# Split values written by 16 transfers of full rows; the inverse's transposes and the first preparation's sums tied to places in TensorE's row

## The chip, the cores and the metric

The kernel runs on one core of a Trainium2 chip. The metric is the device time of one execution in microseconds (us). Runs of one kernel agree to about 0.2%, some 3 us here.

## What is computed

One layer of a diffusion backbone: 1024 latent tokens and 256 context tokens, width 1024, batch 1. The normalised, modulated tokens go through one input projection, whose columns feed two groups; their outputs are projected back, and a SwiGLU network follows.

```python
px = modulate(rms_norm(x, norm1_w), sh1, sc1) @ w_in      # latent
pc = modulate(rms_norm(ctx, norm1_w), csh1, csc1) @ w_in  # context
# group A: gated DeltaNet, 4 heads of 128, forward and backward, chunks of 64
qkv = short_conv(p[..., :3 * DN_WIDTH], conv_w)           # 5 taps, then SiLU
m = jnp.where(strict, jnp.einsum("bhncd,bhnmd->bhncm", kb, k) * decay, 0.0)
a_mat = jnp.eye(CHUNK) + m
u = triangular_solve(a_mat, v * beta); w = triangular_solve(a_mat, kb * jnp.exp(gam))
qk = jnp.where(tril, jnp.einsum("bhncd,bhnmd->bhncm", q, k) * decay, 0.0)
# ... scan over the chunks, then per-head rms_norm * silu(z)
# group B: 8 heads of 64, windows of 8 rows x 16 columns on a 64-wide grid, plus all context keys
s = jnp.concatenate([s_win, s_ctx], axis=-1)
o = softmax(s) @ (v of the window and of the context)
x = x + g1 * (jnp.concatenate([dn_x, na_x], axis=-1) @ w_out)
x = x + g2 * swiglu(modulate(rms_norm(x, norm2_w), sh2, sc2), w_ffn_in, w_ffn_out)
```

## The kernel before

**Products.** Operands in float32 are split into a high and a low part, and each product is three: high by high, low by high, high by low. The tokens' parts are `hh` and `hl`, a weight's `whi` and `wlo`. ACT casts a weight's high part, POOL subtracts to get the low one (L198 and L199 for a block; L584 and L585 for a wide job).

**Jobs.** The input projection is a list of jobs. A *block* computes 128 columns of one kind with columns on partitions: k, q, v of group A (with convolution and SiLU) or nk, nq of group B. For each of 8 slices of the width it issues three products for two or three segments of tokens (L404, up to 512 tokens each). Its life goes on while later jobs run: evacuation from the accumulators by ACT (L452), the convolution on DVE (L456, L460), SiLU on ACT (L467), norm (sums on TensorE at L485 or L491, then L492, L496, L499), finish (transposes on TensorE at L526 for v, and stores). A *wide* job has tokens on partitions, its weights are loaded in two halves through one raw buffer (`wraw`, one copy; load L583, then L584 and L585), and its products are L592, 24 for a tile of 128 tokens. The kinds are z1, nv0, nv1 and z0. The list is k0 to k3, z1, nk0 to nk2, nv0, nk3, q0 to q3, nq0 to nq3, v0, nv1, v1, v2, v3, z0. The weights of a job are requested while the job before it is traced; z0, the last, runs beside the beginning of group B's attention (scores L302, biases L304, exponential L306, transposes L313, values L323).

**Values.** The nv jobs (two halves of the columns) store the values of group B to `nv_d` in device memory (L603). After each, SP issues 64 transfers that sort them by column block into `vw_d` (L1104), 32 KB each, in pieces of 512 bytes. The attention loads one piece of 1536 bytes per partition for each tile (L277).

**Background.** Python generators step beside the jobs, some steps to a slice. `block_inverses` builds decay tables and inverts the triangular blocks: transposes on TensorE (L870), a back-substitution on DVE (L880 and L882, 30 rounds, then the memset of the diagonal, L885), a pause of some steps, then transposes back (L892, 8 groups of 4, of which two are printed as one row of 8, with copies by ACT at L894), a DVE transpose and a scaling (L900, L903), and stores to `x_d`. Then `preps` prepares 10 chunks for both directions, two of them at a time: tables `rg` on POOL (L952), sums on TensorE (L964, L965), exponential (L968), products with the keys on DVE (L971), copies of 32x32 blocks to `y` on POOL (L974), products L984 and L995 with evacuations by ACT and DVE (L987, L997, L998), stores (L1007).

**What sets the order.** The program is traced once; a scheduler then sets the row in which each engine takes its instructions, by data and by its own estimates of when things are ready, and each engine works its row strictly in order. `tc.keep_in_program_order(x)` holds an instruction behind all that was traced before it on its engine. DMA queues are fed by SP and ACT in their rows too.

Of the kernel before, what the change touches and what calls it, by code (L numbers as in the profile page):

```python
# [88 lines left out]
def hybrid(ctx, tc, a, dbg):  # L89
# [56 lines left out]
    nv_d = dram.tile([T, 512], F32, name="nv_d", tag="nv_d")  # L146
    nq_d = dram.tile([NAH, 2, ND, L], F16, name="nq_d", tag="nq_d")
    nk_d = dram.tile([2, NAH, ND, T], F16, name="nk_d", tag="nk_d")
    vw_d = dram.tile([128, 4, 4, 4, 128], F32, name="vw_d", tag="vw_d")
    y_d = dram.tile([2, NCH, 128, 4, 128], F32, name="y_d", tag="y_d")  # L150
    at_d = dram.tile([2, 8, 128, 4, 128], F32, name="at_d", tag="at_d")
    x_d = dram.tile([128, 2, 2, NU, 32], F32, name="x_d", tag="x_d")
# [100 lines left out]
    def attention(nw):  # L253
# [20 lines left out]

        def values(hp, half, cb):
            vw = nw.tile([128, 3, 128], F32, name="vw", tag="vw", bufs=3)
            sp.dma_start(vw, vw_d[:, hp, cb, half:half + 3])  # L277
            return vw

        def context(hp):  # L280
# [93 lines left out]
    with ExitStack() as bs:  # L374
# [445 lines left out]
        def block_inverses():  # L820
            with ExitStack() as gs:
# [61 lines left out]
                    yield  # L883
                flat = N.rearrange("p b r c -> p b (r c)")
                dve.memset(flat[:P, :, 0:1024:33], 1.0)  # L885
                for _ in range(4):
                    yield
                U = WK.rearrange("p d u i -> p (d u) i")
                for i0 in range(0, 32, 4):
                    p = bank()  # L890
                    for i in range(4):
                        pe.transpose(p[:, i * P:(i + 1) * P], N[:P, :, :, i0 + i].rearrange("p b r -> p (b r)"),  # L892
                                     ident[:P, :P])
                    act.copy(U[:, :, i0:i0 + 4], p[:, :4 * P].rearrange("p (i u) -> p u i", i=4))  # L894
                    if i0 % 8 == 4:
                        yield
# [15 lines left out]
        def preps():  # L912

            first_half.close()
            with ExitStack() as gs:
                pk = pools(gs, "pk", "left")
                shift(gs, "ppad", "left", 64)
                pp = pools(gs, "pp", "left")

                def work(name, bufs=2, dt=F32):  # L920
                    return (pk if name == "kk" else pp).tile([128, 4, 128], dt, name=name, tag=name, bufs=bufs)

                fxs = [work(f"fx{d}", 1) for d in range(2)]
                ys = [[work(f"y{d}{i}", 1) for d in range(2)] for i in range(2)]
                for t in fxs + ys[0] + ys[1]:
                    pool.memset(t, 0.0)
                q32 = [slice(b * 32, b * 32 + 32) for b in range(4)]

                def fetch(i):

                    got = []
                    for d in range(2):
                        c = ORDER[d][i]
                        kk, xc = work("kk", 6), pp.tile([128, 2, 4, 32], F32, name="xc", tag="xc", bufs=4)
                        sp.dma_start(kk, kk_d[:, c])
                        sp.dma_start(xc, x_d[:, d, :, c * 4:c * 4 + 4])
                        at = None
                        if c >= 2:
                            at = work("at", 4)
                            sp.dma_start(at, qk_d[:, c - 2])  # L940
                        got.append((d, c, kk, xc, at))
                    return i, got

                def prep(i, got):
                    y = ys[i % 2]
                    rgs = []
                    for d, c, kk, xc, at in got:
                        mle = M[C_LE + d].rearrange("p (o i) -> p o i", o=1).to_broadcast([128, 4, 128])
                        for gg in (GH, GL):
                            rg = work("rg", 4, F32R)  # L950
                            g = gg.bitcast(F32)[:, d, c].rearrange("p (h o) -> p h o", o=1).to_broadcast([128, 4, 128])
                            pool.tensor_tensor(rg, g, mle, OP.mult)  # L952
                            rgs.append(rg)
                    for d, c, kk, xc, at in got:
                        for q in q32:
                            act.copy(fxs[d][q, :, q], xc[q, 1])
                    yield 1
                    if i == 0:
                        yield 1
                    es = []  # L960
                    for d, c, kk, xc, at in got:
                        p = bank("pr")
                        for j in range(2):
                            pe.matmul(p, mr[:, d], fl(rgs[2 * d + j]), start=j == 0, stop=False)  # L964
                        pe.matmul(p, mr[:, 4], mneg[:, d].rearrange("p (o i) -> p o i", o=1).to_broadcast(  # L965
                            [128, 4, 128]), start=False, stop=True)
                        e = work("e", 2)
                        act.activation(fl(e), p, AF.Exp)  # L968
                        es.append(e)
                    for (d, c, kk, xc, at), e in zip(got, es):  # L970
                        dve.tensor_tensor(kk, kk, e, OP.mult)  # L971
                    for (d, c, kk, xc, at), e in zip(got, es):
                        for q in q32:
                            pool.tensor_copy(y[d][q, :, q], xc[q, 0])  # L974
                        if at is not None:
                            dve.tensor_tensor(at, at, e, OP.mult)
                            stores.append((at_d[d, c - 2], at, tick[0] + 2))
                    yield 1
                    yield 1
                    ps = []  # L980
                    for d, c, kk, xc, at in got:
                        p = bank("pr")
                        for h in range(4):
                            pe.matmul(p[:, hs[h]], kk[:, h], fxs[d][:, h], start=True, stop=True)  # L984
                        ps.append(p)
                    for (d, c, kk, xc, at), p in zip(got, ps):
                        act.copy(fl(kk), p)  # L987
                    yield 1
                    for n in range(1, 4):
                        blk = (q32[3 - n], q32[n])  # L990
                        cols = (slice(128 - 32 * n, 128), slice(0, 32 * n))
                        ps = [bank("pr").rearrange("p (h i) -> p h i", h=4) for _ in got]
                        for h in range(4):
                            for (d, c, kk, xc, at), p in zip(got, ps):
                                pe.matmul(p[blk[d], h, :32 * n], kk[:, h, blk[d]], y[d][:, h, cols[d]],  # L995
                                          start=True, stop=True)
                        dve.tensor_copy(y[0][blk[0], :, cols[0]], ps[0][blk[0], :, :32 * n])  # L997
                        act.copy(y[1][blk[1], :, cols[1]], ps[1][blk[1], :, :32 * n])  # L998
                        yield 1
                    for d, c, kk, xc, at in got:  # L1000
                        stores.append((y_d[d, c], y[d], tick[0] + 1))

                stores, tick = [], [0]

                def flush(n):
                    while stores and stores[0][2] <= n:
                        sp.dma_start(*stores.pop(0)[:2])  # L1007

                todo = list(range(NCH))
                live, landing = [], []  # L1010
                while live or todo or landing:
                    if not landing and todo and (todo[0] < 2 or all(x in done for x in queries)):
                        landing.append(fetch(todo.pop(0)))
                    if landing and (not live or len(live) < 2 and live[0][1] >= 4):
                        live.append([prep(*landing.pop(0)), 0])
                    if not live:
                        yield
                    for g in list(live):
                        tick[0] += 1
                        flush(tick[0])  # L1020
                        g[1] += 1
                        if not next(g[0], 0):
                            live.remove(g)
                        yield
                flush(tick[0] + 2)
# [23 lines left out]
        for n in range(2, len(jobs) + 2):  # L1049
# [44 lines left out]
            for _ in fin:  # L1094
                pass
            done.add(n - 2)
            if isinstance(j, Wide) and j.kind == "nv":
                hv = slice(2 * j.half, 2 * j.half + 2)
                vlat = nv_d[CT:].rearrange("(r c) d -> r c d", c=64)
                for cb in range(4):  # L1100
                    for ch in range(4):
                        for r in range(4):
                            rows = vlat[4 * ch + r, BLKS[cb]:BLKS[cb] + 32].rearrange("c (h d) -> c h d", d=128)
                            sp.dma_start(vw_d[r * 32:r * 32 + 32, hv, cb, ch], rows[:, hv])  # L1104
            if nrm:
                nrm.norm()
            if isinstance(j, Block):
# [665 lines left out]
```

## Time and profile before

| | us |
|---|---|
| median of three runs (1541.44 to 1543.45) | 1541.6 |
| the profiled execution | 1541.49 |
| its span, first to last instruction | 1539.4 |
| mean granted TensorE clock | 0.988 |
| PE waiting for DVE at the statistics of the start (L717) | 9.9 |
| transfers L1104: issued from 215.4 to 521.3 | 128 of some 0.6 each |

The profile is of one execution. PE is TensorE, DVE VectorE, ACT ScalarE, POOL GpSimd, SP the engine that issues most transfers; the "q" forms are their sequencers. A timeline row gives the start, the time, the engine, line, operation, output and inputs, the tile, the count, and in brackets the idle time before it with what released it. A row of windows gives the busy time of PE, its weight loads, DVE, ACT and POOL, then the granted clock of TensorE (1.00 is full), the transfer engines' busy share and GB/s. A row of waits gives the total, the number and the longest.

### The profile page before, as it was taken

What the parts mean: (1) busy time and instruction counts of PE and PEld (TensorE: products, weight loads), DVE (VectorE), ACT (ScalarE), POOL (GpSimd) and SP (SyncE); (2) the same over time, 40 slices, a digit from 0 to 9 for tenths busy, and PEclk for the clock granted to TensorE, in tenths of its full rate; (3) what the DMA queues carried; (4) which work ended last, traced back from release to release, by engine and by line L of the source; (5) the groups of instructions that cost most, each with busy time, mean ns of one, the idle gap of its engine ahead of it and who ended that gap; (6) DMA issues with size and microseconds to landing.
All of it is one profiled execution on the core that took longest, in us unless ns stands there. A gap on an engine that the chain in (4) does not pass through costs nothing. (4 is left out here: it accounts for less than half of the span.)

```text
span 1539.4 us, 24029 instructions
## 1 busy us (share of the span) xinstructions
PE 1474.1 (96%) x8702; PEld 1231.0 (80%) x8702; DVE 993.6 (65%) x1712; ACT 728.2 (47%) x1405; POOL 234.8 (15%) x286
## 2 busy tenths in 40 slices
PE   6999998899899898999999999999999999999999
PEld 3788797777688787788888878888888888888887
DVE  4774587974464354677977379855555566599652
ACT  5442552646764236666873176333333334354440
POOL 1054500634554100111210000000000000000000
PEclk9999999999999999999999999999999999999999
DMA  9274232687655557898638503533333334798742
GB/s 387 68 212 139 60 86 79 202 239 246 182 172 170 147 142 247 278 292 253 209 90 282 183 34 109 186 106 106 107 105 103 104 102 148 248 376 275 247 143 82
DMA packets 205142, 267.36 MB, mean 174 GB/s; under 512 B 17760, under 2 KB 115552, under 8 KB 204000
## 3 DMA queue, kind: packets, MB, share of 16 engines
q1 hardware_dynamic: 194320, 258.45, 52.4%
q10 hardware_dynamic: 10704, 7.38, 1.5%
q8 instruction: 68, 1.11, 0.3%
q14 instruction: 50, 0.41, 0.1%
HBM read 201.02 MB, written 68.94 MB: 175 GB/s over the span
## 5 line engine op out<-in xcount | busy, mean ns | idle before, releaser
L404 PE MATMUL blk<-hh,whi 128*128 128x512 f32 (+1 forms) x410 | 123.0, 394 | 6.8 <-ACT cr L452 5.3
L1410 ACT CAST uhi<-ws 128x512 fp32r<-128x512 f32 x91 | 54.0, 621 | 146.0 <-PE ps L1349 96.1
L1410 ACT CAST uhi<-wq 128x512 fp32r<-128x512 f32 x101 | 61.0, 622 | 130.9 <-issue 84.6
L404 PE MATMUL blk<-hl,whi 128*128 128x512 f32 (+1 forms) x410 | 115.4, 375 | 0.3 <-DVE hl L704 0.3
L404 PE MATMUL blk<-hh,wlo 128*128 128x512 f32 (+1 forms) x410 | 114.6, 375 | 0.6 <-POOL wlo L199 0.6
L592 PE MATMUL blk<-zw,hh 128*128 128x256 f32 (+1 forms) x576 | 113.5, 291 | 1.1 <-ACT cr L452 1.0
L1411 DVE TENSOR_TENSOR ulo<-wq,uhi 128x512 fp32r<-128x512 f32 x101 | 67.5, 687 | 58.4 <-ACT uhi L1410 32.4
L1349 PE MATMUL ps<-hT,uhi 128*128 128x512 f32 x336 | 103.6, 390 | 0.0
L1349 PE MATMUL ps<-lT,uhi 128*128 128x512 f32 x336 | 103.5, 389 | 0.0
L1349 PE MATMUL ps<-hT,ulo 128*128 128x512 f32 x336 | 103.4, 389 | 0.0
L592 PEld LDWEIGHTS blk<-zw,hh 128*128 128x128 f32 x576 | 91.7, 191 | 4.0 <-ACT cr L452 1.5
L1349 PE MATMUL ps<-hB,uhi 128*128 128x512 f32 x288 | 89.2, 391 | 0.6 <-ACT hB L1524 0.6
L1349 PE MATMUL ps<-lB,uhi 128*128 128x512 f32 x288 | 88.8, 389 | 0.4 <-DVE lB L1525 0.4
L1349 PE MATMUL ps<-hB,ulo 128*128 128x512 f32 x288 | 88.6, 389 | 0.0
L404 PEld LDWEIGHTS blk<-hh,whi 128*128 128x128 f32 x410 | 69.0, 194 | 21.9 <-ACT cr L452 6.1
L404 PEld LDWEIGHTS blk<-hl,whi 128*128 128x128 f32 x410 | 72.5, 192 | 14.9 <-DVE hl L704 0.8
L404 PEld LDWEIGHTS blk<-hh,wlo 128*128 128x128 f32 x410 | 72.5, 192 | 14.9 <-POOL wlo L199 0.9
L592 PE MATMUL blk<-zw,hl 128*128 128x256 f32 (+1 forms) x288 | 82.4, 286 | 0.0
L199 POOL TENSOR_TENSOR wlo<-wraw,whi 128x1024 fp32r<-128x1024 f32 x18 | 46.6, 2586 | 194.1 <-ACT whi L198 193.9
L1349 PEld LDWEIGHTS ps<-lT,uhi 128*128 128x128 f32 x336 | 63.1, 188 | 13.2
L1349 PEld LDWEIGHTS ps<-hT,ulo 128*128 128x128 f32 x336 | 63.1, 188 | 13.2
L1349 PEld LDWEIGHTS ps<-hT,uhi 128*128 128x128 f32 x336 | 62.9, 188 | 12.9
(362 smaller groups left out, 3526.1 us busy)
## 6 DMA issues: line engine op xcount, KB each, us to landing
wq<-w_fo SPq DMA_DIRECT2D x99, 256.0 KB, 4.1
wq<-w_gu SPq DMA_DIRECT2D x88, 256.0 KB, 2.9
wad<-wa SPq DMA_DIRECT2D x64, 256.0 KB, 4.2
bt<-rpb SPq DMA_DIRECT2D x64, 192.0 KB, 3.7
t_d<-g SPq DMA_DIRECT2D x22, 512.0 KB, 3.7
fr<-t_d SPq DMA_DIRECT2D x44, 256.0 KB, 5.2
f_d<-g SPq DMA_DIRECT2D x33, 256.0 KB, 2.1
fr<-f_d SPq DMA_DIRECT2D x33, 256.0 KB, 4.2
```

What stands on the lines that cost most here:

```text
L199: lo_engine.tensor_tensor(o, r, h.bitcast(F32), OP.subtract)
L404: pe.matmul(o, ww[:, k], xx[k][:, s], start=k == 0 and j == 0, stop=k == KT - 1 and j == 2)
L592: pe.matmul(p[:, :c1 - c0], x[k][:, s], ww[:, k, c0:c1], start=k == 0 and j == 0, stop=k == KT - 1 and j == 2)
L1349: pe.matmul(o, w[wi][:, k], x[xi][:, k], start=first and k == 0 and j == 0, stop=k == n - 1 and j == 2, skip_group_check=True)
L1410: act.copy(hi, self.raw[key])
L1411: dve.tensor_tensor(lo, self.raw[key], hi.bitcast(F32), OP.subtract)
```

## The change

Three parts:

- `vw_d` is laid out with full rows of 512 columns, and written after the second nv job alone, by 16 transfers of 256 KB, each row 2 KB. The attention's load of a tile takes three pieces of 512 bytes per partition.
- In `block_inverses` the pause before the transposes back is 6 steps where it was 4, and the first transpose of each group of four is held in program order.
- In `preps` the first preparation waits 10 steps (LATE) where it waited 1, its sums are held in program order, and its count of steps starts at -10, so that the second preparation does not begin sooner against it.

```diff
-    vw_d = dram.tile([128, 4, 4, 4, 128], F32, name="vw_d", tag="vw_d")
+    vw_d = dram.tile([128, 4, 4, 512], F32, name="vw_d", tag="vw_d")
...
-            sp.dma_start(vw, vw_d[:, hp, cb, half:half + 3])
+            sp.dma_start(vw, vw_d[:, cb, half:half + 3, hp * 128:hp * 128 + 128])
...
                 dve.memset(flat[:P, :, 0:1024:33], 1.0)
-                for _ in range(4):
+                for _ in range(6):
                     yield
...
-                        pe.transpose(p[:, i * P:(i + 1) * P], N[:P, :, :, i0 + i].rearrange("p b r -> p (b r)"),
-                                     ident[:P, :P])
+                        t = pe.transpose(p[:, i * P:(i + 1) * P], N[:P, :, :, i0 + i].rearrange("p b r -> p (b r)"),
+                                         ident[:P, :P])
+                        if not i:
+                            tc.keep_in_program_order(t)
...
-                    if i == 0:
+                    for _ in range(LATE if i == 0 else 0):
                         yield 1
...
-                            pe.matmul(p, mr[:, d], fl(rgs[2 * d + j]), start=j == 0, stop=False)
+                            m = pe.matmul(p, mr[:, d], fl(rgs[2 * d + j]), start=j == 0, stop=False)
+                            if i == 0:
+                                tc.keep_in_program_order(m)
...
-                stores, tick = [], [0]
+                LATE, stores, tick = 10, [], [0]
...
-                        live.append([prep(*landing.pop(0)), 0])
+                        live.append([prep(*landing.pop(0)), 0 if live or len(todo) < NCH - 1 else -LATE])
...
-            if isinstance(j, Wide) and j.kind == "nv":
-                hv = slice(2 * j.half, 2 * j.half + 2)
-                vlat = nv_d[CT:].rearrange("(r c) d -> r c d", c=64)
+            if isinstance(j, Wide) and n == values:
+                vlat = nv_d[CT:].rearrange("(n r c) d -> r c n d", r=4, c=64)
                 for cb in range(4):
-                    for ch in range(4):
-                        for r in range(4):
-                            rows = vlat[4 * ch + r, BLKS[cb]:BLKS[cb] + 32].rearrange("c (h d) -> c h d", d=128)
-                            sp.dma_start(vw_d[r * 32:r * 32 + 32, hv, cb, ch], rows[:, hv])
+                    for r in range(4):
+                        sp.dma_start(vw_d[r * 32:r * 32 + 32, cb], vlat[r, BLKS[cb]:BLKS[cb] + 32])
```

Lines behind the diff's places move by up to 4: the copies L894 become L896, the sums L964 become L966.

On TensorE, in block q0, the transposes back (`m<-cst,N`) among q0's products (`hh_134` is slice 3, `hh_451` slice 4, up to `hh_457`, slice 7). Before:

```order
L404 MATMUL blk<-hh_134,wlo 128x512 x2
L892 MATMUL m<-cst,N 128x80 x8
L404 MATMUL blk<-hh_451,whi 128x512 x2
L404 MATMUL blk<-hl_452,whi 128x512 x2
L404 MATMUL blk<-hh_451,wlo 128x512 x2
L892 MATMUL m<-cst,N 128x80 x8
```

And in the changed kernel, where the third and fourth groups are shown too:

```order
L404 MATMUL blk<-hh_453,wlo 128x512 x2
L892 MATMUL m<-cst,N 128x80 x8
L404 MATMUL blk<-hh_455,whi 128x512 x2
L404 MATMUL blk<-hl_456,whi 128x512 x2
L404 MATMUL blk<-hh_455,wlo 128x512 x2
L892 MATMUL m<-cst,N 128x80 x8
...
L892 MATMUL m<-cst,N 128x80 x8
L491 MATMUL pr<-cr,cst 128x512
L491 MATMUL m<-cr,cst 128x256
L491 MATMUL m<-cr,cst 128x512
L404 MATMUL blk<-hh_128,whi 128x512 x2
```

The first group stands two slices later, and the fourth (behind the rows shown) comes after the three L491 sums of nk3's norm; before, all four came ahead of them.

On ACT, at the end of the v blocks: `zw<-wraw` is the cast of a half of z0's weights, `cr<-blk` a block's evacuation, `cacc<-cacc` its SiLU. Before (the evacuations are of v1, v2 and v3):

```order
L452 COPY cr<-blk 128x256
L452 COPY cr<-blk 128x512 x2
L584 CAST zw<-wraw 128x8x128
L467 ACT_TABLE_LOAD
L467 ACTIVATE cacc<-cacc 128x1280
L452 COPY cr<-blk 128x256
L452 COPY cr<-blk 128x512 x2
L467 ACTIVATE cacc<-cacc 128x1280
L584 CAST zw<-wraw 128x8x128
L534 DMA v_d<-vt 128x10x128
L452 COPY cr<-blk 128x256
L452 COPY cr<-blk 128x512 x2
```

And in the changed kernel (the evacuations shown are of v2 and v3):

```order
L452 COPY cr<-blk 128x512 x2
L467 ACTIVATE cacc<-cacc 128x1280
L534 DMA v_d<-vt 128x10x128
L452 COPY cr<-blk 128x256
L452 COPY cr<-blk 128x512 x2
L467 ACTIVATE cacc<-cacc 128x1280
L584 CAST zw<-wraw 128x8x128
L306 ACT_TABLE_LOAD
L306 ACTIVATE bt,mx<-bt,mx 128x640
L584 CAST zw<-wraw 128x8x128
```

Both casts stood ahead of v3's evacuation; now they stand behind v3's SiLU, with the attention's first exponential between them.

On TensorE behind v3's last product: before, the products L592 of z0 followed it directly, 72 of them. In the changed kernel 16 score products of the attention come first, of which the row shows the last; then z0's first four among the transposes of the softmax (`sc<-cst,bt`):

```order
L404 MATMUL blk<-hh_457,wlo 128x512 x2
...
L302 MATMUL sc<-kl,qs 128x384
L313 MATMUL sc<-cst,bt 128x128 x2
L592 MATMUL blk<-zw,hh_128 128x256
L592 MATMUL blk<-zw,hl_129 128x256
L592 MATMUL blk<-zw,hh_128 128x256
L592 MATMUL blk<-zw,hl_129 128x256
L313 MATMUL sc<-cst,bt 128x128 x3
L302 LDWEIGHTS qs
L302 MATMUL sc<-kh,qs 128x256
L592 MATMUL blk<-zw,hh_128 128x256
```

The first two transposes L313 wait for the first exponential, the first L592 for both casts, and the fifth for POOL's low part.

## The prediction

> **What bounds the kernel now.** I read the busy times, then TensorE's waits, then the stretches in which those waits fall: timelines of PE and of the engine named, and the busy times by window.
>
> ```profile
> span 1539.4 us, 24029 instructions
> PE 1474.1 (96%) x8702; PEld 1231.0 (80%) x8702; DVE 993.6 (65%) x1712; ACT 728.2 (47%) x1405; POOL 234.8 (15%) x286
> ```
>
> PE is busy for 96% of the span, so only PE's idle time (1539.4 - 1474.1 = 65.3 us) and its slow-clock time can change. The waits of PE, in us in total, times and longest:
>
> ```profile
> PE pr L995 <- ACT kk L987: 7.3, 6, 2.1
> PE m L892 <- DVE N L885: 5.7, 1, 5.7
> PE blk L404 <- ACT cr L452: 5.3, 1, 5.3
> PE pr L964 <- POOL rg L952: 2.7, 4, 0.9
> PE pr L984 <- DVE kk L971: 1.1, 1, 1.1
> ```
>
> Three of them are where the change reaches: the inverse's transposes (A, L892), the first preparation's sums (B, L964 with L984), and the wait of a block's first product for the evacuation before it (C, L404 behind L452). Each is longer than its idle time, because the granted clock falls after it. The windows (PE, PEld, DVE, ACT, POOL busy, then the clock) after A, in B, and after C, and one after a short wait elsewhere:
>
> ```profile
> 255.90:262.65 6.75, 4.16 (x15) 3.24 (x16) 2.83 (x8) 0.85 (x2) 0.00 (x0) 0.50 0.19 49
> 293.30:300.10 6.80, 5.80 (x16) 4.13 (x17) 6.69 (x7) 1.78 (x3) 6.68 (x6) 0.51 1.00 311
> 444.00:447.00 3.00, 3.00 (x20) 2.71 (x19) 3.00 (x4) 2.88 (x8) 1.67 (x2) 0.50 0.75 216
> 532.66:539.07 6.41, 4.56 (x13) 3.79 (x14) 4.50 (x8) 2.77 (x5) 1.39 (x1) 0.50 1.07 257
> ```
>
> Half of PE's busy time at clock 0.50 is lost: 2.1 us after A, 2.9 in B, 2.3 after C.
>
> **Part A, the transposes.** The changed row has 12 more L404 products (128x512) ahead of the first L892 group, and 6 between the groups as before, but the fourth group now comes behind nk3's three L491 sums.
>
> ```profile
> 251.44 0.62 PE L404 MATMUL blk<-hl,whi 128*128 128x512 f32 x2
> 251.89 0.61 PE L404 MATMUL blk<-hh,wlo 128*128 128x512 f32 x2
> 258.17 0.53 PE L892 MATMUL m<-cst,N 80*128 80x80 f32 x2 [5.66 <-DVE N L885]
> 259.03 1.06 PE L892 MATMUL m<-cst,N 80*128 80x80 f32 x6 [0.33 <-DVE N L882]
> ```
>
> Two products take 251.89 - 251.44 = 0.45 us from start to start, so 12 fill 2.73 of the 5.66 + 0.33 = 6.0 us; 3.3 us stay, since DVE's substitution sets their end and is not moved. DVE itself loses 0.79 us upstream, where it waits for ACT, and ACT for a transfer of the split values after the first nv job:
>
> ```profile
> 225.41 1.55 DVE L499 SCALAR_TENSOR_TENSOR cacc<-cacc,qkw,cr 128x1280 f32<-128x1280 f32 x1 [0.79 <-ACT cr L496]
> 219.86 1.28 ACT L492 ACT_TABLE_LOAD   x1 [3.09 <-DMA vw_d<-nv_d]
> ```
>
> Those 64 transfers are gone, so up to 0.79 comes on top: I take 3.0 of idle time removed (2.7 to 3.5). The fourth group is new behind ACT: its banks are those that L491 writes and L492 reads, and L492 stands behind two evacuations and a table load.
>
> ```profile
> 270.13 1.07 ACT L452 COPY cr<-blk 128x512 f32<-128x512 f32 x2
> 271.21 1.28 ACT L492 ACT_TABLE_LOAD   x1
> 272.51 1.05 ACT L492 ACTIVATE cr<-m,bias 128x256 f32<-128x256 f32 x2
> 273.45 0.69 ACT L492 ACTIVATE cr<-pr,bias 128x512 f32<-128x512 f32 x1
> ```
>
> ACT needs 1.07 + 1.28 + 1.05 + 0.69 = 4.1 us for this after the third group's copies; PE meanwhile has 6 products (1.4 us) and the sums (some 0.4), so 2.3 us of waiting at most, 0.9 where the first 256 columns suffice for the first bank (a third of the 1.05: 1.07 + 1.28 + 0.35 - 1.8). I take 1.8 back. The clock: 2.1 us were lost; the remaining gap of some 2.5 to 3.3 us is nearest to this one, ahead of the third window above:
>
> ```profile
> 443.05 0.41 PE L995 MATMUL pr<-y,kk 128*32 128x32 f32 x8 [2.07 <-ACT kk L987]
> ```
>
> There 2.07 us of idling brought 3 us at 0.50, a loss of 1.5. So 0.6 to 2.1 is saved, 1.0 taken. A: 3.0 - 1.8 + 1.0 = **2.2 us gained** (bounds 2.7 - 2.3 + 0.6 = 1.0 and 3.5 - 0.9 + 2.1 = 4.7).
>
> [...]
>
> **Part B, the first sums.** The four L964 sums stood 76 products behind the transposes' fourth group and stand 97 behind it now, with a second L485 and two L548 groups ahead of them: 21 x 0.23 = 4.8 us and some 2 us for these, so POOL's four rg tables should be nearly done when PE comes to them. What is lost there before:
>
> ```profile
> 291.77 0.50 PE L964 MATMUL pr<-rg,mr 128*128 128x512 f32 x1 [0.94 <-POOL rg L952]
> 296.00 4.62 POOL L974 COPY y<-xc 32x128 f32<-32x128 f32 x4
> L585 POOL TENSOR_TENSOR zw<-wraw,zw x8: 2351/2402/2852, 82.8 to 544.7; 128x1024 fp32r<-128x1024 f32 x6, 128x1088 fp32r<-128x1088 f32 x2
> ```
>
> Waits of 2.7 + 1.1 and 2.9 by the clock make 6.7 us. What is late next is POOL: in the changed row a weight's low part (L199, the same shape as the L585 of 2.40 us) stands between the first and the second y copies (4.62 us), so the second direction's products L995 come up to 2.4 us late; the inverse, whose last group waits in part A, delays its tables on DVE and POOL too, and the sums wait for the first rg still (0.94 as now, and about as much for L485 behind ACT). 2.4 + 0.94 + 0.9 = 4.2, with a little clock 4.7. **B gains 2.0** (bounds: all 6.7; minus 3 where POOL's 4.62 of copies and 2.4 both show with their slow clock).
>
> **Part C, the split values.** In front of z0's first weights SP issues 64 small transfers:
>
> ```profile
> 490.92 30.98 SPq L1104 DMA_DIRECT2D vw_d<-nv_d  x46
> 530.57 1.05 ACT L584 CAST zw<-wraw 128x1024 fp32r<-128x1024 f32 x1 [13.89 <-DMA wraw<-w_z]
> 534.51 0.80 PE L404 MATMUL blk<-hh,whi 128*128 128x512 f32 x1 [5.32 <-ACT cr L452]
> ```
>
> ACT, in order, waits at L584 for that load, so v2's evacuation stands behind it and PE idles for 5.32 us: with 2.3 of slow clock 7.6 us. Sixteen transfers at the same 0.67 us (30.98/46) take 11 us on SP instead of 43, and L584 now stands later; the wait goes, and some hand-over stays (no other such L404 wait in the waits, 1.03 at z0's start): 0.4. **Gain 7.2.**
>
> But the changed order moves more. On ACT both L584 casts of z0's weights are now behind v3's evacuation and its silu (L467), the second even behind the attention's first exponential; they were ahead of v3's evacuation. SP's second load of w_z waits for the raw buffer (one only), so for POOL's L585 of the first half. On PE z0's first product needs both casts, the third product of each k POOL's low part. All this starts only when v3's products end, at 551.16 + 0.75 = 551.91:
>
> ```profile
> 551.16 0.75 PE L404 MATMUL blk<-hh,wlo 128*128 128x256 f32 x3
> 552.94 0.38 PE L592 MATMUL blk<-zw,hh 128*128 128x256 f32 x1 [1.03 <-ACT cr L452]
> 553.92 5.90 DVE L460 SCALAR_TENSOR_TENSOR cacc<-cr,cw,cacc 128x255 f32<-128x255 f32 x6
> 559.86 1.28 ACT L467 ACTIVATE cacc<-cacc 128x1280 f32<-128x1280 f32 x1 [0.55 <-DVE cacc L460]
> DMA to landing us min/median/max: 3.4/4.4/6.0
> L302 PEld LDWEIGHTS <-qs x320: 95/98/100, 565.5 to 796.9; 128*128 128x128 f16 x160
> ```
>
> (The row on landing is that of L583.) Counted from 551.91: the convolution ends at +7.9 and silu at +9.2; the first cast (1.05) at +10.3; POOL's L585 (2.40) at +12.7; the second load (4.4) at +17.1; its cast at +18.1, POOL's part at **+20.5**. Today z0 starts at +1.03. PE has little to do meanwhile: 17 score products of the attention, 5 transposes and z0's first four, 26 in all; each brings a weight load of 0.1 us, beside which its product runs, so 2.7 (6.0 at most, at the 0.23 of a 512-wide product, which none of them exceeds). So 20.5 - 1.0 - 2.7 = 16.8 us are lost, and as after C's old gap 2.3 by the clock: **19.1 lost**. Today the casts hide behind v2's and v3's products; with that cover gone they cost their full chain.
>
> The values are now read in three pieces of 512 bytes per partition, where one of 1536 was. I cost it at nothing: the first use comes some 27 us after z0's old start, and the copies of before were themselves in 512-byte pieces. Bounds: 0 and 8 (a rival, below).
>
> **The sum.** The profiled execution took 1541.49, its span 1539.4 with 2.1 around it; the median of the runs is 1541.6, so both serve. 1541.5 - 2.2 - 2.0 - 7.2 + 19.1 = **1549 us**, slower; its own range 1543 to 1555 by the bounds (the landing 3.4 to 6.0, B's two ends, the work pulled forward).
>
> **Rivals.**
>
> *The attention sets the end, not z0.* During the long wait DVE and ACT begin the attention's softmax: the first exponential would start some 12 us behind v3's end, at 564, and not behind z0's first tiles. PE waits for that chain later, in all:
>
> ```profile
> PE sc L313 <- DVE bt L308: 3.4, 4, 1.8
> PE sc L302 <- DVE mx L304: 3.3, 4, 1.6
> PE sc L323 <- ACT pt L316: 3.2, 6, 1.0
> PE sc L313 <- ACT pt L316: 1.9, 5, 0.6
> PE sc L313 <- DVE mx L304: 1.4, 2, 1.0
> ```
>
> If the lead holds through the stage, these 13.2 us are given back and the time is 1549 - 13.2 = 1536, faster (0.12); if it holds for the first half of the stage only, some 7 come back and it is 1542, no change (0.13). The mechanism decides from 10.5 us given back on. Against it: PE's row behind z0's first 72 products is nearly the old one, and by the first values' product (L323) as much attention has been issued as before, so the lead is one or two tiles of softmax.
>
> *It does not do what it says* (0.15): L892 and L964 are later, but DVE's substitution and POOL's tables slip with them, so A and B gain nothing: 1541.5 - 7.2 + 19.1 = 1553.
>
> *The smaller pieces* (0.05). In the attention the transfer engines' share (the last but one number) is high:
>
> ```profile
> 593.00:603.00 10.00, 6.92 (x59) 5.21 (x60) 7.48 (x16) 8.19 (x18) 0.94 (x3) 1.00 0.92 304
> ```
>
> If each of the 32 loads of values lands a quarter microsecond later on the path, 8 us come on top: 1557. [...]
>
> **How the numbers follow.** My forecast has 0.55. A measurement of this kernel tells about 0.2%, 3.1 us, from no change: faster is under 1538.5, slower over 1544.7. Slower: 0.52 of the forecast's 0.55, and 0.15 and 0.05: 0.72. Same: the half given back and the forecast's lowest end, 0.13 + 0.03. Faster: 0.12. The range 1538 to 1556 takes in all but the full give-back and the smaller pieces.
>
> **What would show it.** Between v3's last L404 and z0's third L592 PE idles for 15 to 19 us, in the waits put down to POOL's L585 or ACT's L584, with the clock at 0.50 after it; the wait of L404 behind L452 is gone or under 1 us; L892's wait is 2.5 to 3.3 us; L964 waits for little. I am wrong if z0's products start within 10 us of v3's end, or if the attention's waits shrink by most of their 13.2 us.

## The result, and the profile after

The changed kernel takes 1551.96 us (median of four, 1549.18 to 1552.19); the kernel before took 1541.52 beside it. The ratio is 1.0068, 95% interval [1.0054, 1.0082]: slower, by some 10 us. The profiled execution of the changed kernel took 1549.18 and is the fastest of its four, so the traces account for 7.9 us of span (1547.3 - 1539.4), not for the whole median.

The first lines of the page of the changed kernel:

```profile
span 1547.3 us, 23913 instructions
PE 1478.8 (96%) x8702; PEld 1235.7 (80%) x8702; DVE 991.7 (64%) x1712; ACT 731.9 (47%) x1407; POOL 234.5 (15%) x286
```

PE's busy time grew by 4.7 us with the same 8702 instructions, which is slow clock (0.982 granted on the mean, 0.988 before), and its idle time by 3.2 (68.5 where 65.3 were). PE's waits, in us in total, times and longest:

```profile
PE sc L302 <- DMA kh<-nk_d: 8.1, 1, 8.1
PE pr L999 <- ACT kk L991: 8.1, 6, 2.1
PE sc L302 <- DVE mx L304: 6.2, 4, 3.8
PE sc L313 <- DVE bt L308: 5.2, 5, 1.8
...
PE m L485 <- ACT cr L470: 3.1, 1, 3.1
PE m L892 <- DVE N L885: 2.1, 1, 2.1
```

The 5.3 us of L404 behind L452 are gone, and so are the waits of the first sums (L964, now L966; L995 and L987 are L999 and L991). L892's wait fell from 5.7 to 2.1. New are 8.1 us for a load of the attention's keys, 3.1 us of L485, and 4.7 more behind the softmax (6.2 and 5.2, where 3.3 and 3.4 were).

To see where these fall, I cut both spans at four events on PE that both traces have: the second L851 (rc, with a wait of 1.75) at 169 us, the first product of the prepared chunks with a wait of 2.01 (L999 at 393; L995 at 397 before), v3's last product, and z0's last. The table also shows three of the experiments below.

| stretch, us | before | changed | without C | loads free | z0 early |
|---|---|---|---|---|---|
| start to the L851 | 169.4 | 168.9 | 168.7 | 169.0 | 170.1 |
| to the L999 (parts A and B) | 227.8 | 224.1 | 223.7 | 224.8 | 222.2 |
| to v3's end (part C) | 154.7 | 147.1 | 154.9 | 147.3 | 146.8 |
| to z0's end | 31.7 | 48.7 | 31.7 | 45.3 | 32.0 |
| to the end of the span | 955.8 | 958.5 | 955.0 | 958.1 | 957.9 |

A and B together gained 3.7 us, C 7.6, z0 lost 17.0. The last stretch lies between 955.0 and 959.8 in all eleven traces, 957.6 in one without part C. Its 2.7 us are slow clock: from 606 to 613 the changed kernel's PE was busy for 5.98 us at clock 0.52, some 2.9 us lost, where the kernel before kept 1.00 from 585 to 640. All seven kernels with part C fall below full clock between 585 and 640 (0.91 to 0.97, the changed one 0.94), and one of the four without it (0.97); whether C brings this about was not tested.

**Part A.** PE's timeline at the transposes, and the windows after them (PE, PEld, DVE, ACT, POOL busy, clock):

```profile
256.65 0.45 PE L892 MATMUL m<-cst,N 80*128 80x80 f32 x2 [2.07 <-DVE N L885]
257.51 0.97 PE L892 MATMUL m<-cst,N 80*128 80x80 f32 x6 [0.41 <-DVE N L882]
268.77 0.67 PE L892 MATMUL m<-cst,N 80*128 80x80 f32 x4 [0.45 <-ACT cr L492]
```

```profile
258.00:264.00 6.00, 6.00 (x31) 5.05 (x31) 0.00 (x0) 2.56 (x5) 0.00 (x0) 0.72 0.01 3
```

The gap was 5.66 + 0.33 and is 2.07 + 0.41; the fourth group, whose banks ACT must first read, waits 0.45. After the short gap the clock is still low: 0.72 over 6 us, 1.7 us lost.

**Part B.** The sums wait for nothing now, but another wait stands in front of them, at the sums of q1's norm (the second L485). DVE's row shows what has moved: two tables of the inverse, a transposition (L902) and a scaling (L905), 1.5 us each, have come between the steps of q1's convolution (L460). That they are not the whole cause is shown by part B alone, below.

```profile
290.20 1.50 DVE L902 STREAM_TRANSPOSE ut<-WK 128x1280 f32<-128x1280 f32 x1
291.63 1.24 DVE L460 SCALAR_TENSOR_TENSOR cacc<-cr,cw,cacc 128x1023 f32<-128x1023 f32 x1
292.79 1.49 DVE L905 TENSOR_TENSOR WK<-WK,NB 128x1280 f32<-128x1280 f32 x1
294.19 1.28 DVE L460 SCALAR_TENSOR_TENSOR cacc<-cr,cw,cacc 128x1022 f32<-128x1022 f32 x1
```

```profile
295.51 1.06 ACT L467 ACTIVATE cacc<-cacc 128x1024 f32<-128x1024 f32 x1 [4.41 <-DVE cacc L460]
296.60 1.06 ACT L470 ACTIVATE cr<-cacc 128x1024 f32<-128x1024 f32 x1
```

```profile
297.70 2.36 PE L485 MATMUL m<-ones,cr 128*128 128x1 f32 x16 [3.13 <-ACT cr L470]
```

```profile
297.60:304.00 6.40, 6.29 (x26) 5.42 (x27) 4.89 (x6) 4.42 (x9) 6.20 (x8) 0.61 0.81 250
```

The convolution ends, ACT takes its SiLU and squares, and PE gets its sums 3.13 us late, with 6.4 us at clock 0.61 behind.

**Part C and z0.** SP's timeline, then what SP's queue waited for between 500 and 560 us:

```profile
487.77 13.87 SPq L1105 DMA_DIRECT2D vw_d<-nv_d  x16
501.82 1.53 SPq L1011 DMA_DIRECT2D at_d<-at  x2
503.68 4.48 SPq L1011 DMA_DIRECT2D y_d<-y  x4
540.77 0.61 SPq L583 DMA_DIRECT2D wraw<-w_z  x1
...
552.73 0.59 SPq L583 DMA_DIRECT2D wraw<-w_z  x1
```

```profile
SPq L583 <- DMA v_d<-vt: 32.5, 1, 32.5
```

ACT, POOL and PE from v3's end (540.08) to z0:

```profile
537.05 0.38 ACTq L534 DMA_DIRECT2D v_d<-vt  x1
539.71 1.35 ACT L452 COPY cr<-blk 128x256 f32<-128x256 f32 x3 [5.79 <-PE blk L404]
548.08 1.27 ACT L467 ACTIVATE cacc<-cacc 128x1280 f32<-128x1280 f32 x1 [7.02 <-DVE cacc L460]
549.25 1.03 ACT L584 CAST zw<-wraw 128x1024 fp32r<-128x1024 f32 x1
...
556.87 1.05 ACT L584 CAST zw<-wraw 128x1024 fp32r<-128x1024 f32 x1 [1.05 <-DMA wraw<-w_z]
```

```profile
550.36 2.34 POOL L585 TENSOR_TENSOR zw<-wraw,zw 128x1024 fp32r<-128x1024 f32 x1 [35.84 <-ACT zw L584]
557.99 2.37 POOL L585 TENSOR_TENSOR zw<-wraw,zw 128x1024 fp32r<-128x1024 f32 x1 [5.29 <-ACT zw L584]
```

```profile
548.21 0.59 PE L302 MATMUL sc<-kh,qs 128*128 128x256 f16 x2 [8.13 <-DMA kh<-nk_d]
...
554.63 0.37 PE L302 MATMUL sc<-kh,qs 128*128 128x256 f16 x1 [3.78 <-DVE mx L304]
...
557.63 0.66 PE L313 MATMUL sc<-cst,bt 128*128 128x128 f32 x2 [1.78 <-DVE bt L308]
...
560.41 0.79 PE L592 MATMUL blk<-zw,hh 128*128 128x256 f32 x2 [0.37 <-POOL zw L585]
```

```profile
540.00:548.20 8.20, 0.08 (x1) 0.02 (x1) 7.73 (x10) 1.18 (x4) 0.00 (x0) 0.79 0.78 203
548.20:560.40 12.20, 6.12 (x26) 3.73 (x26) 4.72 (x10) 7.44 (x11) 4.75 (x3) 0.50 0.97 264
```

The chain is the one that was forecast: convolution, SiLU, cast, POOL's low part, second load, cast, POOL. PE has 26 products for 20.3 us. The new thing is on SP. Its queue was free at 508.2. Until 513.5 the first load of z0's weights would have waited anyhow, for POOL's low part of v3's weights (L199, which ends at 513.52): in the kernels below in which no store holds it, it leaves when L199 ends. Yet it left at 540.77. The trace puts 32.5 us of SP's waiting down to the completion of a *store* that ACT issued at 537.05, v1's values to `v_d` (L534), with which the load shares no data. The traces show why. In both, the transfers of SP and ACT signal their landing on the same eight semaphores, the counters 0 to 7 below, taken in turn. No transfer was issued before the last one on its counter had landed, in 934 repeats of a counter in the changed kernel and 1046 before; z0's first load was issued 0.06 us behind that landing (times in us):

```
                         counter, use  issued   use before it  landed
before   z0's 1st load      0, 50      525.45         49       522.79
         z0's 2nd load      7, 51      536.65         50       536.59
         v1's store (ACT)   0, 53      548.89         52       542.86
changed  v1's store (ACT)   1, 35      537.05         34       500.35
         z0's 1st load      1, 36      540.77    35, v1's store 540.71
         z0's 2nd load      0, 38      552.73         37       550.44
```

With 112 transfers fewer, 14 turns of eight, and z0's loads traced as before, the store now precedes the first load on its counter. SP's wait for the semaphore that the two share stands at 540.72 in the changed kernel, just ahead of the load.

### The profile page after: what moved, and what is told of

It is laid out like the page before. It is cut to its first block, busy times and chain, and to the rows that moved or that the text cites. A ratio compares the mean times of both kernels' runs of the same rounds, so it can differ in the third digit from the quotient of the medians.

```text
span 1547.3 us, 23913 instructions
## 1 busy us (share of the span) xinstructions
PE 1478.8 (96%) x8702; PEld 1235.7 (80%) x8702; DVE 991.7 (64%) x1712; ACT 731.9 (47%) x1407; POOL 234.5 (15%) x286
## 3 DMA queue, kind: packets, MB, share of 16 engines
q1 hardware_dynamic: 194576, 258.44, 51.6%
## 5 line engine op out<-in xcount | busy, mean ns | idle before, releaser
L404 PE MATMUL blk<-hh,whi 128*128 128x512 f32 (+1 forms) x410 | 123.7, 395 | 1.5 <-ACT kk L549 1.4
L592 PE MATMUL blk<-zw,hh 128*128 128x256 f32 (+1 forms) x576 | 114.1, 292 | 1.6 <-ACT kk L549 1.1
L404 PE MATMUL blk<-hl,whi 128*128 128x512 f32 (+1 forms) x410 | 115.2, 376 | 0.3 <-DVE hl L704 0.3
L404 PE MATMUL blk<-hh,wlo 128*128 128x512 f32 (+1 forms) x410 | 114.0, 375 | 0.6 <-POOL wlo L199 0.6
L1412 DVE TENSOR_TENSOR ulo<-wq,uhi 128x512 fp32r<-128x512 f32 x101 | 67.6, 688 | 58.7 <-ACT uhi L1411 32.5
L592 PEld LDWEIGHTS blk<-zw,hh 128*128 128x128 f32 x576 | 92.3, 192 | 5.1 <-ACT kk L549 1.4
L404 PEld LDWEIGHTS blk<-hh,wlo 128*128 128x128 f32 x410 | 72.6, 192 | 15.2 <-POOL wlo L199 0.9
L404 PEld LDWEIGHTS blk<-hl,whi 128*128 128x128 f32 x410 | 72.3, 192 | 14.8 <-DVE hl L704 0.8
L592 PE MATMUL blk<-zw,hl 128*128 128x256 f32 (+1 forms) x288 | 82.7, 287 | 0.0
L404 PEld LDWEIGHTS blk<-hh,whi 128*128 128x128 f32 x410 | 68.7, 193 | 16.8 <-issue 4.0
L199 POOL TENSOR_TENSOR wlo<-wraw,whi 128x1024 fp32r<-128x1024 f32 x18 | 45.0, 2501 | 197.3 <-ACT whi L198 179.5
```

The lines of the kernel that those rows point to most:

```text
L199: lo_engine.tensor_tensor(o, r, h.bitcast(F32), OP.subtract)
L404: pe.matmul(o, ww[:, k], xx[k][:, s], start=k == 0 and j == 0, stop=k == KT - 1 and j == 2)
L592: pe.matmul(p[:, :c1 - c0], x[k][:, s], ww[:, k, c0:c1], start=k == 0 and j == 0, stop=k == KT - 1 and j == 2)
L1412: dve.tensor_tensor(lo, self.raw[key], hi.bitcast(F32), OP.subtract)
```

## The experiments

All comparisons are with the kernel before, run on the same chip.

**One part alone, and all but one.** The first question was whether the loss is C's alone, and how A and B add up. In the first of these four the edits of A and B are undone; in the second those of B and C; in the third of A and C; in the fourth of C:

```diff
 # A undone
-                for _ in range(6):
+                for _ in range(4):
...
-                        if not i:
-                            tc.keep_in_program_order(t)
 # B undone
-                    for _ in range(LATE if i == 0 else 0):
+                    if i == 0:
...
-                            if i == 0:
-                                tc.keep_in_program_order(m)
...
-                        live.append([prep(*landing.pop(0)), 0 if live or len(todo) < NCH - 1 else -LATE])
+                        live.append([prep(*landing.pop(0)), 0])
 # C undone
-    vw_d = dram.tile([128, 4, 4, 512], F32, name="vw_d", tag="vw_d")
+    vw_d = dram.tile([128, 4, 4, 4, 128], F32, name="vw_d", tag="vw_d")
...
```

> Only the split values' part of the change (layout, 16 transfers); the transposes and the first sums stand as before. If the three parts add up, this lacks the 3.7 us that the two traces show gone by the first preparation (397.2 against 393.0, less 0.5 of the start) and is some 3 to 4 us slower than the changed kernel: 1555. z0's first main product still comes 20 us behind v3's end, and the wait of L404 behind L452 is gone. Rival: the two other parts give their gain back later (then it is as the changed kernel, 1552), or it is they that move z0's casts (then the time is under 1541).

> Only the transposes back, of the kernel before: 6 steps of pause, first of each group in program order. By the prediction 2.2 us gained (1 to 4.7); by the trace of the changed kernel, idle 6.0 down to 2.9 and the clock back sooner, 3.5: 1538. Rival: the sums behind them take it back, since the tables of x come later: 1541 or more.

> Only the first preparation's sums, of the kernel before: ten steps and program order. By the prediction 2.0 gained. By the trace of the changed kernel, where a wait of 3.1 us at L485 and its slow clock took the place of the waits at L964: about 0, 1541. If the wait at L485 comes from the later transposes (their tables on DVE fall into q1's convolution), it is not there when the transposes stand as before, and the gain is 4 to 6: 1536.

> The transposes and the sums together, the split values as before (128 transfers). The traces' difference by the first preparation less that of the start is 3.7 us: 1538. SP is busy with its transfers again, so the wait of L404 behind L452 (5.3 us) is back, z0's casts stand ahead of v3's evacuation, and z0 starts 1 us behind v3's end. Rival: the loss at z0 comes from the other two parts, and z0 is late here too: over 1550.

| kernel | us | before | ratio, 95% interval | second stretch |
|---|---|---|---|---|
| C alone | 1549.77 | 1542.69 | 1.0052 [1.0035, 1.0069] | 228.3 |
| A alone | 1542.27 | 1541.97 | 1.0000 [0.9982, 1.0018] | 226.6 |
| B alone | 1544.17 | 1541.97 | 1.0010 [0.9995, 1.0026] | 229.4 |
| A and B | 1537.90 | 1541.97 | 0.9979 [0.9966, 0.9992] | 223.7 |

C alone is slower by 0.52% and has the 32.5 us of SP's waiting, so the late z0 is C's. A and B without C are 0.21% faster (some 3.2 us by the ratio), and L404's wait is back. On top of C the gain of A and B shows in the two traces only: C alone was expected at 1555, some 3 us behind the changed kernel, and took 1549.77, and the two ratios, 1.0052 and 1.0068, cannot be told apart. C alone's profiled execution (1552.75) was the slowest of its four, the changed kernel's the fastest of its four.

A and B are not a sum of two: alone, A brings 1.5 us in the second stretch and B loses 1.3 (against 228.1, the mean of before and of C alone), together they bring 4.4. In time, A alone was expected at 1538 and brought nothing, as its rival had it. Each alone has the late L485, A alone and then B alone:

```profile
301.42 3.06 PE L485 MATMUL m<-ones,cr 128*128 128x1 f32 x16 [3.13 <-ACT cr L470]
```

```profile
305.61 3.57 PE L485 MATMUL m<-ones,cr 128*128 128x1 f32 x16 [4.10 <-ACT cr L470]
```

So the wait at L485 comes whichever of the two is moved, and with both it comes once. In B alone DVE's tables stand where they stood before the change (L900 at 280.60, L903 at 284.59), and ACT takes q1's convolution at 302.27, hardly later than the 301.73 of before. PE comes to L485 earlier instead: at 301.5, where it came at 311.7. The forecast that the wait would be gone without A's later tables failed.

**The counter, or the rows?** z0's casts stand behind v3's SiLU on ACT; SP waits for a counter. Which of the two makes z0 late? The first kernel shifts the rotation by one, with one of the sixteen transfers cut in two; the second holds v3's evacuation behind z0's second cast on ACT; the third does both.

```diff
 # rotation shifted by one
-                        sp.dma_start(vw_d[r * 32:r * 32 + 32, cb], vlat[r, BLKS[cb]:BLKS[cb] + 32])
+                        for s in ((slice(0, 2), slice(2, 4)) if cb * 4 + r < 1 else (slice(0, 4),)):
+                            sp.dma_start(vw_d[r * 32:r * 32 + 32, cb, s], vlat[r, BLKS[cb]:BLKS[cb] + 32, s])
 # casts ahead of v3's evacuation
-                    act.copy(self.hi[:, :, s], r)
+                    self.cast = act.copy(self.hi[:, :, s], r)
...
-                j.evac()
+                with tc.issue_after(jobs[n + 1].cast.ins) if n == len(jobs) - 2 else ExitStack():
+                    j.evac()
```

> The changed kernel with one of its 16 transfers cut in two, so that the 17 shift all later transfers by one completion counter; z0's first weights no longer share one with the store of v_d. Theory of the counter: SP held that load for 32.5 us behind v_d's store; freed, it is issued by 510, and if this alone makes z0 late, z0 starts within 2 us of v3's end: about 1533. Theory of the rows: the casts still stand behind v3's evacuation, the second one behind the attention's first exponential, so with the load there at once z0 starts some 14.5 us behind v3's end (exponential at +12.5, cast, POOL 2.4) and not 20: 1546.

> The changed kernel with both of z0's casts tied ahead of v3's evacuation on ACT; the 16 transfers and the shared counter stay. Theory of the rows: that puts z0 where it was, within 2 us of v3's end, 1533. Theory of the counter: the load is still issued only behind v_d's store at some 541, lands at 545, the second half (POOL, load, cast) is ready at 556, and now v3's evacuation waits behind the casts too: z0 starts 13 to 16 us behind v3's end: 1545 to 1549.

> Both edits: 17 transfers, and the casts ahead of v3's evacuation. If counter and rows together are the cause, the load is early, both casts are done before v3 ends, z0 starts about 1 us behind v3's end, and 17 us of the traces' difference at z0's end, up to 19, are gone: 1533 (1531 to 1536), faster than both kernels. If neither is the cause, z0 stays late and the time over 1545.

| kernel | us | ratio, 95% interval (before: 1542.69) | v3's end to z0's end |
|---|---|---|---|
| rotation shifted | 1547.93 | 1.0036 [1.0024, 1.0048] | 46.5 |
| casts ahead | 1551.25 | 1.0063 [1.0043, 1.0083] | 51.6 |
| both | 1547.53 | 1.0044 [1.0027, 1.0061] | 50.2 |

Shifted, z0's first load left at 516.98, as soon as POOL was done with v3's weights, but then the transfer that came next into the store's counter, a load of the attention's queries (L259), stood in its place, and SP with it:

```profile
SPq L259 <- DMA v_d<-vt: 26.6, 1, 26.6
```

z0's second load is behind that one on SP, so z0 gained 2.2 us only; the time is near the 1546 of the rows' theory and far from the 1533 of the counter's. With the casts ahead, ACT waits for the loads and PE for the evacuation behind the casts, 18.6 us, more than the 13 to 16 that were expected if the counter is the cause:

```profile
558.66 0.58 PE L592 MATMUL blk<-zw,hh 128*128 128x256 f32 x1 [18.61 <-ACT cr L452]
```

Here my first theory fell: "both" was to bring 1533, and brought 1547.5. Its waits have the same 26.5 us at L259, and the second load left at 544.94, behind fourteen other transfers of SP. The store takes one of the eight counters seen above, so by their turn one of SP's next eight new transfers should meet it, whichever that is; shifting the rotation moved the stall to a neighbour (26.6 and 26.5 us at L259). The load should be free only if nothing that meets the store stands ahead of it.

**Loads free, rows left.** So the next kernel frees both loads: five of the sixteen transfers are cut in two, z0's weights are requested one job earlier, and the attention's first loads are held behind z0's second load. The casts stay where the scheduler puts them, now ahead of v3's SiLU.

```diff
-                        sp.dma_start(vw_d[r * 32:r * 32 + 32, cb], vlat[r, BLKS[cb]:BLKS[cb] + 32])
+                        for s in ((slice(0, 2), slice(2, 4)) if cb * 4 + r < 5 else (slice(0, 4),)):
+                            sp.dma_start(vw_d[r * 32:r * 32 + 32, cb, s], vlat[r, BLKS[cb]:BLKS[cb] + 32, s])
...
-                next(fill)
+                with tc.issue_after(jobs[-1].load.ins):
+                    next(fill)
...
-            if n + 1 < len(jobs):
+            if n + 1 < len(jobs) - 1:
...
+            if n == len(jobs) - 3:
+                jobs[-1].prefetch()
```

> The changed kernel with five of the sixteen transfers of the split values cut in two (21 in all), and the attention's first loads behind z0's second load on SP, so that neither of z0's loads shares its completion counter with v1's late store. The casts stand where the scheduler then puts them: behind v3's evacuation but ahead of its silu on ACT, and on PE z0's products stand right behind v3's. Theory (the loads' waiting is one half, the casts' and the single raw buffer's place in the rows the other): SP's 26 to 33 us of waiting for v_d's store are gone, the first cast runs at about +2.5 us from v3's end, POOL's low part at +4.9, the second load lands at +9.3 and z0's third product of a k waits for POOL until about +12.8; z0's main start is 7 to 8 us earlier than the changed kernel's +20.3, and the time 1542 to 1546. Rival (the counter alone made z0 late): with both loads free z0 starts within 3 us of v3's end and the time is 1531 to 1535. Second rival (the counter costs nothing, only the rows): z0 starts at +18 to +21 and the time is 1548 to 1552.

Measured: 1543.67 us (before: 1540.37), ratio 1.0015 [0.9995, 1.0036]. SP's waits, ACT's casts and PE, with v3's end at 541.12:

```profile
SPq L583 <- POOL zw L585: 26.7, 1, 26.7
```

```profile
541.97 1.07 ACT L584 CAST zw<-wraw 128x1024 fp32r<-128x1024 f32 x1
550.15 1.05 ACT L584 CAST zw<-wraw 128x1024 fp32r<-128x1024 f32 x1 [7.11 <-DMA wraw<-w_z]
```

```profile
553.68 0.80 PE L592 MATMUL blk<-zw,hh 128*128 128x256 f32 x2 [1.21 <-POOL zw L585]
```

The store is no longer among SP's waits; what SP waits for now is the raw buffer, whose first half POOL frees only after a cast that stands behind v3's evacuation. z0's third product starts 12.6 us behind v3's end (12.8 expected, 20.3 in the changed kernel). So both are at work: the counter makes the first load, and with it the casts, late; the casts' row and the one raw buffer make the rest. As SP's order of loads was changed too, the 7.7 us that z0 starts earlier are not the counter's alone. Of these 7.7 us only 3.4 show in the trace's stretch (45.3 for 48.7): in the changed kernel PE did 3 us of the attention's products in the gap, and its slow clock fell into it; here it had none to do, and z0's own products ran at 0.50 (553.6 to 556.6). The ratios differ by more, 0.53%, with intervals of 0.15 to 0.2% on each side; the runs of this kernel spread from 1535 to 1549, so the size is known less well than the place.

**z0's work all under v1 to v3.** The last kernel removes both causes: z0's loads are traced one job earlier and the attention's held behind them, v1's and later stores wait behind the second cast, and the evacuations of v2 and v3 stand behind one cast each, v3's also behind v2's SiLU.

```diff
-                    (act if kind == "v" else sp).dma_start(dst[:, i * 128:(i + 1) * 128].rearrange("(c p) d -> p c d", p=128), vt)
+                    with tc.issue_after(jobs[-1].cast[1].ins) if kind == "v" and i else ExitStack():
+                        (act if kind == "v" else sp).dma_start(dst[:, i * 128:(i + 1) * 128].rearrange("(c p) d -> p c d", p=128), vt)
...
-                next(fill)
+                with tc.issue_after(jobs[-1].load.ins):
+                    next(fill)
...
-                j.evac()
+                with tc.issue_after(jobs[-1].cast[n - len(jobs) + 3].ins) if len(jobs) - 3 <= n < len(jobs) - 1 else ExitStack():
+                    with tc.issue_after(jobs[n - 1].gate.ins) if n == len(jobs) - 2 else ExitStack():
+                        j.evac()
```

> The changed kernel with z0's weights requested one job earlier and tied: both loads ahead of the attention's loads on SP, the first cast ahead of v2's evacuation, the second ahead of the store of v_d and of v3's evacuation. No load of z0 then stands behind a transfer that shares a counter with v_d's store. Theory of the counter in SP's order (what the four runs before point to: in each SP stood 26 to 32 us for v_d's store, and z0's second load behind it): both halves are ready before v3 ends, z0 starts about 1 us behind v3's end and the 15 to 20 us between v3's end and z0's end are gone: 1533 (1530 to 1536), faster than both kernels. Rival, that z0 is late by something else (its row on TensorE, or the three-piece loads on the transfer engines): it stays over 1543.

Measured: **1531.24 us** (before: 1541.97), ratio 0.9936 [0.9916, 0.9957], faster than both. ACT and PE (L584 is L586 here, L592 is L594):

```profile
522.92 1.03 ACT L586 CAST zw<-wraw 128x1024 fp32r<-128x1024 f32 x1
523.85 1.35 ACT L452 COPY cr<-blk 128x256 f32<-128x256 f32 x3
530.48 1.05 ACT L586 CAST zw<-wraw 128x1024 fp32r<-128x1024 f32 x1 [5.27 <-DMA wraw<-w_z]
530.54 0.38 ACTq L535 DMA_DIRECT2D v_d<-vt  x1
```

```profile
540.51 0.39 PE L594 MATMUL blk<-zw,hh 128*128 128x256 f32 x1 [1.38 <-ACT cr L452]
```

z0 starts 1.38 us behind v3's end and its stretch is back at 32.0, while C's 7.9 and A's and B's 5.6 us stay. The store's counter still holds a load on SP, one of the attention's (L282, 4.7 us), but z0's loads have left by then.

## Why the prediction was right

The time lies 3 us over the forecast of 1549 and inside its own range. The profiled execution, 1549.18, is on it, in part by luck: z0's loss was forecast 2.1 us too large, and the last stretch, for which the sum has no term, cost 2.7. By the steps:

- **z0 late, the largest term: the chain as forecast, 19.1 us against 17.0.** The chain was to bring z0's main products at +20.5; they came at +20.3 (560.41 - 540.08). The 2.3 us for the clock was hardly lost on top: the stretch at 0.50 lies inside the wait (548.2 to 560.4), and the 3 us behind it, at 0.75, cost 0.7. z0's whole stretch grew by 19.3 less the 2.3 that the work pulled forward saved.
- **Two of its signs came out otherwise.** PE idled for 14.2 of the 20.3 us, where 15 to 19 were named, and the trace puts this down to the attention's keys and softmax (8.13, 3.78 and 1.78), only 0.37 to POOL: the attention's products stand first in PE's row, and their keys' loads stood behind z0's held load on SP. And L892 waited 2.07 us, not 2.5 to 3.3.
- **What the step lacked was the cause of the late casts.** The prediction took it from the changed rows that the casts stand behind v3's SiLU, and did not ask why, nor what SP does between 508 and 541. It named the raw buffer alone as what holds a load. The first load was held to 540.8, some 27 us longer than by POOL's L199, by a counter that it shares with v1's store. That both causes count is shown by the experiments with the loads freed (12.6 us left) and with all of it moved (1.38).
- **C: 7.2 forecast, 7.6 measured**, and 9.0 with C alone (154.7 to 145.7). L404's wait is gone whole, and nothing stands in its place on PE before v3's end.
- **A and B: 4.2 forecast, 3.7 measured** between the two traces, 4.3 from the means of the seven traces with both and the two with neither (223.71 and 228.05). The split was off, and that its two errors nearly cancel is luck. *A was sized too small:* the fourth group was to give 1.8 us back and gave 0.45, so idle time fell by 5.99 - 2.93 = 3.1; the clock gave 0.4 (2.1 lost before, 1.7 now) for 1.0 forecast: 3.5 in place of 2.2. *B was sized too large, by a wrong place:* it was to lose its cover at POOL's copies in front of the second direction's products; in fact the wait moved to L485, 3.1 us, and 2.5 of clock, with some 1.0 more at 0.76 until 308, so that B's 6.7 came back nearly whole. "About as much for L485 behind ACT", 0.9 us, was the term that was a third of the truth.
- **The rivals.** The attention gave hardly anything back: behind z0's start, its waits are nearly what they were (from z0's first products to 800, L313 behind L308 waits 3.4 in both traces, L302 behind L304 2.5 after 3.3), so the lead of one or two tiles was used up at once. A and B did what they say in the traces, and in the runs without C. The smaller pieces of the values cost nothing: the loads land in 3.7 us by the median after 3.8.

```profile
vw<-vw_d SPq DMA_DIRECT2D x32, 192.0 KB, 3.7
```

## What to carry to other kernels

A transfer can wait for one with which it shares no data, when both use the same completion counter (some 27 us here); so when transfers are added or removed, look at what SP's queue waits for right behind the place, before looking at the engines. When small transfers that held up a load are taken away, check that the load moves up: whatever else was timed by the old delay (here a cast, a store, a raw buffer) must be moved with it. A wait removed from PE's row is worth what the next thing in that row leaves of it: A and B were each worth nothing alone and 0.21% together.

## What the hardware showed that was not expected

**A load held for some 27 us by a store on another engine's queue,** in five kernels: SP waited 32.5 us in the changed kernel, with C alone and with the casts ahead, 26.6 and 26.5 with the rotation shifted. Of the 32.5 in the changed kernel the first 5 would have gone by anyhow, and 513.5 to 540.8 are the store's.

**The same gap, with and without a slow clock.** At the inverse's transposes the kernels with A wait for the same DVE work. After 2.07 us the changed kernel ran at 0.72 for 6 us; the kernel with z0 early, whose instructions there are the same, waited as long and lost nothing:

```profile
257.85 0.45 PE L894 MATMUL m<-cst,N 80*128 80x80 f32 x2 [2.06 <-DVE N L887]
```

```profile
258.00:264.00 6.00, 5.59 (x36) 4.92 (x37) 0.58 (x3) 2.77 (x6) 0.00 (x0) 1.00 0.01 3
```

Of six profiled kernels with gaps of 2.06 to 2.08 us there, four fell to 0.50 within 4 us and two kept 1.00. The slow stretches of these traces are 3.41 us long or a multiple of it (258.11 to 261.52 in the changed kernel, 255.84 to 262.66 in the kernel before), with every edge of a trace on one grid of 3.41 us in these two, and in the six kernels it mattered where the gap fell in that grid. In the changed kernel PE was busy for 1.04 us of the 3.41 from 254.70 to 258.11, and the next 3.41 ran at 0.50; in the three others that slowed it was busy for 1.35, 1.42 and 1.59 us of the stretch ahead. Where the clock stayed, a boundary of the grid cut the gap: PE was busy for 1.71 and then 2.63 us with z0 early, 1.63 and 2.72 in the kernel with the shifted rotation and the casts ahead.

So some 1.7 us of part A's worth is luck from one trace to the next.
